# Low parts of every fourth weight chunk by an adding transfer, and a 128-row low part of the rotary key

## The chip, the cores and the metric

The kernel runs on one core of a Trainium2 chip. The metric is the device time of one execution in microseconds (us). A core has a matmul engine (TensorE, PE in the rows; its weight loads are PEld), VectorE (DVE), ScalarE (ACT), GpSimd (POOL) and SyncE (SP, which here only issues loads); 16 DMA engines move data between HBM and the on-chip memory SBUF. Matmuls write to PSUM, from where VectorE or ScalarE take the result.

## The reference

A two-layer encoder trunk on 256 tokens of width 2048, all in float32. Cut to what matters:

```python
for l in range(DEPTH):                                   # DEPTH = 2
    proj = rms_norm(x, attn_norm[l]) @ w_in[l]           # 2048 x 4928
    aq, ak, av, bq, bk, bv, cq, ckv, ckr = split(proj)
    ya = dense_block_attention(rope(aq), rope(ak), av)   # 6 heads, 2 key heads
    yb = dilated_mixture(rope(bq), rope(bk), bv)         # 4 heads, 3 patterns
    q  = rms_norm(cq) @ w_uq[l]                          # 6 heads, 128 + 64 rotary columns
    kv = rms_norm(ckv) @ w_ukv[l]                        # 6 heads, 128 key + 128 value columns
    k  = concatenate([k_nope, broadcast(apply_rope(ckr))])   # one rotary key of 64 for all heads
    yc = dense_block_attention(q, k, cv)                 # scores over 192 columns
    x  = x + concatenate([norm(ya), norm(yb), norm(yc)]) @ w_out[l]
    x  = x + conv_ffn(rms_norm(x), w_up[l], ..., w_down[l])  # 2048 -> 2 x 5632 -> 2048
return rms_norm(x, final_norm)
```

## The kernel before

**Two parts for each operand.** TensorE multiplies in float32r, which keeps fewer bits than float32. So each operand is held as a high part (the value rounded to float32r) and a low part (value minus high part), and a product is made of three: high x high, high x low, low x high. Activations live in `pg` tiles (high and low side by side), weights in `wh` and `wl`.

**Weight chunks.** All weights of both layers are streamed through the core once, in 802 chunks of at most 128 x 1024 numbers (512 KB; most of w_out's and a third of w_down's are 384 KB), in the order of PLAN: w_in (78 chunks a layer), w_ukv, w_uq (11), w_out (40), w_up and w_down (176 and 96, interleaved in four groups). For each chunk there are three steps: `emit_dma` issues the load into a landing tile `wland` on SyncE's queue, `emit_high` casts it to `wh` on ScalarE, `emit_low` subtracts `wh` from `wland` into `wl` on VectorE. Buffers rotate: 5 of wland (LAND), 4 of wh (SPLIT + 1), 3 of wl (SPLIT). Each engine works its queue in order.

**Who is ahead of whom.** `use()` is called when TensorE's code comes to a chunk u. It first calls `prefetch`, which writes out the cast of chunk u+3, the low part of chunk u+2 and the load of the chunk five behind the low parts. The cast of u+3 writes the wh buffer of chunk u−1, and the low part of u+2 the wl buffer of u−1, so both wait for TensorE to be done with that; the load waits for the low part that frees its landing tile.

**How chunks are used.** `rows` (w_in, values, rotary queries): weights are the moving operand, two k-blocks of 512 columns a chunk; the second matmul of a chunk already reads wl. `cols` (w_out, w_down, the 128-wide heads): weights are stationary; for each half of the chunk first all matmuls with wh, then those with wl. `up` (w_up): eight matmuls with wh, then eight with wl. Results go to one of two `mm` accumulators in PSUM.

**The order of the rest.** Everything else (norms, rotary embedding, heads, convolution) is written as generators that `pump` advances between the matmuls of a chunk, when the planner's clock (class Clock, a model of each engine's time) says that what they need is done. `urgent` ones come first, attention heads (`bg`) after them.

**Group C's scores.** `ckr_gen` makes the rotary key: its transposed 64 rows stand twice in the 128 rows of `krh` (high part), while `krl` (low part) has 64 rows. The rotary query tile `qr` has its high part in rows 0 to 63 and its low part in rows 64 to 127. One matmul with krh gives high x high plus low x high; a second one, with the first 64 rows of qr and krl, gives high x low. With the three products of the 128 other columns, that is five matmuls of 256 columns for each head and each block of 128 queries.

**Lines.** All compute instructions are recorded through one helper and carry line 164 (L164); loads carry L270. `rstd` puts a power of −0.5 on GpSimd (tiles `small`), which has little else to do.

Of the kernel before, what the change touches and what calls it, by code (L numbers as in the profile page):

```python
# [14 lines left out]
F32 = mybir.dt.float32  # L15
F32R = mybir.dt.float32r
BF16 = mybir.dt.bfloat16
AF = mybir.ActivationFunctionType
ALU = mybir.AluOpType
AX = mybir.AxisListType  # L20

P = 128
D = 2048
S = 256
# [8 lines left out]
ROPE_C = 64  # L33
# [9 lines left out]
CHUNK = 1024  # L43
# [15 lines left out]
def plan():  # L59
# [3 lines left out]
    def cols(mat, ks, c0, w):  # L63
        for run in k_runs(ks, w):
            out.append((mat, run, c0, w))
# [53 lines left out]
class Clock:  # L119
# [9 lines left out]
    def run(self, engine, cost, outs, ins):  # L129
        start = max([self.at[engine]] + [self.written.get(i, 0.0) for i in ins])  # L130
        end = self.at[engine] = start + cost
        for o in outs:
            self.written[o] = end + self.HOP
        for x in outs + ins:
            self.last[x] = max(self.last.get(x, 0.0), end + self.HOP)
        self.step = max(self.step, end + self.HOP)
# [84 lines left out]
class Kern:  # L221
# [51 lines left out]
        c.written.setdefault(dst.name, c.at["dma"] + 2000.0)  # L273


    LAND, SPLIT = 5, 3

    def emit_dma(self):
        i = self.n_dma
# [11 lines left out]
    def emit_high(self):  # L291
        i = self.n_high
        _, _, nk, w = self.chunks[i]
        sz = nk * w
        h = self.t("wh", [P, CHUNK], self.SPLIT + 1, F32R)
        if i > self.SPLIT:
            self.clock.at["act"] = max(self.clock.at["act"], self.ends[i - self.SPLIT - 1])
        self.ac.copy(h[:, :sz], self.land[i][:, :sz])
        self.high[i] = h
        self.n_high += 1  # L300

    def emit_low(self):
        i = self.n_low
        _, _, nk, w = self.chunks[i]
        sz = nk * w
        lo = self.t("wl", [P, CHUNK], self.SPLIT, F32R)
        h = self.high.pop(i)
        if i >= self.SPLIT:
            self.clock.at["dve"] = max(self.clock.at["dve"], self.ends[i - self.SPLIT])
        self.ve.tensor_tensor(lo[:, :sz], self.land.pop(i)[:, :sz], h[:, :sz].bitcast(F32), ALU.subtract)  # L310
        v = lambda x: x[:, :sz].rearrange("p (k n) -> p k n", k=nk)
        self.parts[i] = (v(h), v(lo))
        self.n_low += 1
# [393 lines left out]
    def attention(self, layer, act, norm):  # L707
# [9 lines left out]
        def uses(n, *tiles):  # L717
            for t in tiles:
                used[id(t)] = [t, n]

        def used_once(*tiles):
            for t in tiles:
                used[id(t)][1] -= 1
                if used[id(t)][1] == 0:
                    self.pg.put(t)
# [9 lines left out]
        qn, qr, kn, vC = {}, {}, {}, {}  # L735
# [26 lines left out]
        def ckr_gen(pm1):  # L762
            while "ckv" not in state:
                yield
            t = state["ckv"]
            self.evac(pm1, t[:, :, 256:], rs[0], 256)
            k = self.t("ckr", [P, NB, 1, ROPE_C], 1)
            self.evac(pm1, k[:, :, 0], rs[0], ROPE_C, 256)
            self.mm.put(pm1)
            yield  # L770
            ss = self.small(2)
            yield from self.sumsq(t, ss)
            tmp, z = yield from self.rope(k, self.c3("cosC"), self.c3("sinC"), 32, True)
            yield
            r = self.rstd(ss, 512, 2)
            yield
            self.scale(t, r)
            yield
            g = vec("c_kv_norm", 4)
            yield from self.transposed(lambda j, b: t[:, b, j * P:(j + 1) * P], 0, ckvT,  # L780
                                       [g[:, j:j + 1] for j in range(4)])
            self.tm.put(t)
            pt = yield from self.take(self.at)
            for b in range(NB):
                self.te.transpose(pt[:, 0, b * P:(b + 1) * P], z[:, b, 0].rearrange("p s d -> p (s d)"), self.ident)
            self.scr.put(tmp)
            yield
            h, lo = self.kr
            self.ac.copy(h, pt[:, 0])
            self.ve.tensor_tensor(lo, pt[:ROPE_C, 0], h[:ROPE_C].bitcast(F32), ALU.subtract)  # L790
            self.at.put(pt)
            kr.append(self.kr)

# [43 lines left out]
        def c_heads():  # L837
            for i in range(3):
                while not (i in qn and i in qr and i in kn and i in vC and kr):
                    yield  # L840
                mine = (*qn[i], qr[i], *kn[i], *vC[i])
                uses(2, *mine)
                (qh, ql), (kh, kl), (rh, rl) = qn[i], kn[i], kr[0]
                for j in range(2):
                    h = 2 * i + j
                    parts = [(x[:, j], y[:, j]) for x, y in ((qh, kh), (qh, kl), (ql, kh))]
                    parts += [(qr[i][:, j], rh), (qr[i][:ROPE_C, j], rl)]
                    self.bg.append(self.head(parts, (HD + ROPE_C) ** -0.5, vC, (i, j), outs["C"], 10 + h,
                                             lambda mine=mine: used_once(*mine)))

# [112 lines left out]
        product(act, K16, 512, lambda pm: a_gen(True, pm))  # L963
        product(act, K16, 256, ckv_gen)
        product(act, K16, 320, ckr_gen)
        product(act, K16, 512, cq_gen, True)
        for hs in ((0, 1), (2,)):
            product(ckvT, K4, 256 * len(hs), lambda pm, hs=hs: vC_gen(hs, pm))
        for i in range(3):
            pm = self.take_mm()  # L970
            self.cols(pm, ckvT, K4, i == 2)
            self.urgent.append(nope_gen(kn, i, pm))
        product(cqT, K4, 384, qr_gen)
        self.urgent.append(c_heads())
        for i in range(3):
            pm = self.take_mm()
# [143 lines left out]
    def run(self):  # L1120
        nc, a = self.nc, self.a
        cp = self.cp
        self.x = [cp.tile([P, 2, S], F32, name=f"x{m}") for m in range(KD // 2)]
        self.cst = cp.tile([P, NCST], F32, name="cst")
        self.vecs = cp.tile([P, DEPTH * NVEC], F32, name="vecs")
        self.mask = cp.tile([P, NB, 512], BF16, name="mask")
        self.load(nc.scalar, self.vecs[:, :64], a["vecs"][:, :64])
        while self.n_dma < self.LAND:
            self.emit_dma()
        self.ident = self.cst[:, CST["ident"]:CST["ident"] + P]  # L1130
        self.ones = self.cst[:, CST["ones"]:CST["ones"] + P]
        self.half = self.cst[:, CST["half"]:CST["half"] + 16]
        self.kr = cp.tile([P, S], F32R, name="krh"), cp.tile([ROPE_C, S], F32R, name="krl")
        self.hs = Fixed(cp.tile([P, 2, S + 2], F32, name=f"hs{i}") for i in range(2))
        for h in self.hs.tiles:
            nc.gpsimd.memset(h[:, :, 0:1], 0.0)
            nc.gpsimd.memset(h[:, :, S + 1:S + 2], 0.0)

        act, norm = {}, self.new_norm()
        first = norm  # L1140
        g0 = VEC["attn_norm"]

        def each(step):
            for m in range(KD // 2):
                yield from step(m)

        self.urgent.append(each(lambda m: self.x_parts(m, act, self.vecs[:, g0:g0 + 16])))
        self.urgent.append(each(lambda m: self.add_squares(first, self.x[m])))
        def tables():
            while self.n_dma < len(self.x) + 1:  # L1150
                yield
            self.load(nc.sync, self.cst, a["cst"])
            self.load(nc.sync, self.vecs[:, 64:], a["vecs"][:, 64:])
            self.load(nc.sync, self.mask, a["mask"].rearrange("p (b k) -> p b k", b=NB))
            self.rope_gains(0)

        self.urgent.append(tables())
        for layer in range(DEPTH):
            if layer:
                self.rope_gains(layer)  # L1160
            self.urgent.append(self.rstd_rows(norm))
            fact, fnorm = self.attention(layer, act, norm)
            act, norm = self.ffn(layer, fact, fnorm, layer == DEPTH - 1)
        self.urgent.append(self.rstd_all(norm, False))
        self.drain(lambda: not self.urgent and not self.bg)
        r = norm.all[0].unsqueeze(1).to_broadcast([P, 2, S])
        for m, x in enumerate(self.x):
            self.ve.tensor_tensor(x, x, r, ALU.mult)
            nc.sync.dma_start(a["out"][m].rearrange("p (j s) -> p j s", j=2), x)
# [94 lines left out]
```

## Time and profile before

| | |
|---|---|
| median of 3 runs | 2286.99 us (2286.73 to 2287.81) |
| profiled execution | 2286.59 us, of which the span from first to last instruction is 2284.8 |
| TensorE busy | 2263.7 us, 99% |
| VectorE busy | 1644.1 us, 72% |
| ScalarE busy | 1217.7 us, 53% |
| GpSimd busy | 32.9 us, 1% |
| loads | 408 MB, 52.4% of the 16 DMA engines' span |

Busy times are sums over the span. Ends of matmuls are modelled and successive matmuls overlap, so the pace of TensorE is read from the starts of its instructions, and what holds it from the waits. A row of the timeline merges equal instructions that follow each other: its first two numbers are the start of the first and the time to the end of the last, xN their count, and in brackets the engine's idle time before it and what ended that.

### The profile page before, as it was taken

To read this page: it belongs to the slowest core of one execution; us is meant where nothing else is said; L and a number is where in the kernel's file an instruction comes from. 1 tells how busy PE (TensorE), PEld (TensorE's weight loads), DVE (VectorE), ACT (ScalarE), POOL (GpSimd) and SP (SyncE) were. 2 spreads that over 40 slices of the span, in tenths; PEclk is the share of its full clock that TensorE was granted. 3 is DMA by queue.
4 is the path that set the end of the run, shared out by engine and by line. 5 is a ranking of instruction groups with operands and counts; after the bars stand their busy time and mean duration, and the time that the engine had idled before them with its cause. 6 is when DMAs were issued, how large, how long until landed. Compare 5 with 4: busy or idle time off the path is not lost. (4 is left out here: it accounts for less than half of the span.)

```text
span 2284.8 us, 34786 instructions
## 1 busy us (share of the span) xinstructions
PE 2263.7 (99%) x13452; PEld 2009.3 (88%) x13452; DVE 1644.1 (72%) x2369; ACT 1217.7 (53%) x1778; POOL 32.9 (1%) x51
## 2 busy tenths in 40 slices
PE   8999999999999999999999999999999999999997
PEld 7889889888888888888988898898888888888897
DVE  6577778777766776776756877787777677667755
ACT  6456745555544554553545566555555455445543
POOL 1000000000000000000010000000000000000000
PEclk9999999999999999999999999999999999999999
DMA  7544435555555555555554444465555555555553
GB/s 275 183 147 149 161 116 189 193 185 191 186 180 198 187 186 190 191 181 186 191 188 173 157 148 140 136 198 185 188 190 184 185 194 191 181 194 191 182 186 121
DMA packets 119110, 410.15 MB, mean 180 GB/s; under 512 B 13344, under 2 KB 13856, under 8 KB 118944
## 3 DMA queue, kind: packets, MB, share of 16 engines
q1 hardware_dynamic: 118800, 407.90, 52.4%
q8 instruction: 105, 1.72, 0.3%
q14 instruction: 61, 0.50, 0.1%
q10 hardware_dynamic: 144, 0.03, 0.0%
HBM read 405.78 MB, written 2.10 MB: 179 GB/s over the span
## 5 line engine op out<-in xcount | busy, mean ns | idle before, releaser
L164 DVE TENSOR_TENSOR wl<-wland,wh 128x1024 fp32r<-128x1024 f32 (+2 forms) x802 | 943.6, 1177 | 497.3 <-PE mm L164 448.0
L164 PE MATMUL mm<-pg,wh 128*128 128x512 f32 (+1 forms) x5472 | 1274.1, 368 | 0.4 <-DVE pg L164 0.4
L164 ACT CAST wh<-wland 128x1024 fp32r<-128x1024 f32 (+2 forms) x802 | 810.7, 1011 | 761.3 <-PE mm L164 399.7
L164 PEld LDWEIGHTS mm<-pg,wh 128*128 128x128 f32 x5472 | 905.6, 190 | 120.0 <-PE mm L164 0.7
L164 PEld LDWEIGHTS mm<-pg,wl 128*128 128x128 f32 x4832 | 690.2, 190 | 60.3
L164 PE MATMUL mm<-pg,wl 128*128 128x256 f32 x4832 | 724.4, 282 | 0.0
L164 PE MATMUL mm<-wh,pg 128*128 128x512 f32 (+3 forms) x1504 | 435.9, 366 | 6.4 <-ACT pg L164 6.4
L164 PEld LDWEIGHTS mm<-wh,pg 128*128 128x128 f32 x1504 | 272.7, 189 | 46.6 <-ACT pg L164 6.4
L164 PE MATMUL mm<-wl,pg 128*128 128x512 f32 (+3 forms) x752 | 272.6, 362 | 0.3 <-DVE wl L164 0.2
L164 DVE SCALAR_TENSOR_TENSOR pp<-hs,vecs,pp 128x256 f32<-128x256 f32 x352 | 162.3, 482 | 6.3
L164 PEld LDWEIGHTS mm<-wl,pg 128*128 128x128 f32 x752 | 142.7, 190 | 19.8 <-DVE wl L164 1.2
L164 DVE TENSOR_TENSOR x<-x,mm 128x512 f32<-128x512 f32 x160 | 109.2, 683 | 6.9 <-PE mm L164 4.7
L164 ACT ACTIVATE pp<-hs,vecs 128x256 f32<-128x256 f32 x176 | 96.2, 594 | 15.5 <-DVE hs L164 15.5
L164 ACT CAST pg<-pp 128x256 fp32r<-128x256 f32 x88 | 35.8, 407 | 89.6 <-DVE pp L164 89.5
L164 ACT ACTIVATE pp<-pp 128x256 f32<-128x256 f32 x88 | 36.9, 419 | 86.7 <-DVE pp L164 86.7
L164 DVE TENSOR_TENSOR pg<-pp,pg 128x256 fp32r<-128x256 f32 x88 | 37.4, 425 | 38.7 <-ACT pg L164 38.7
L164 DVE TENSOR_TENSOR hs<-hs,rall 128x512 f32<-128x512 f32 x88 | 60.9, 692 | 3.1
L164 DVE TENSOR_TENSOR hs<-mm,hs 128x512 f32<-128x512 f32 x88 | 60.1, 683 | 0.0
L164 ACT COPY hs<-mm 128x512 f32<-128x512 f32 x88 | 51.1, 580 | 0.0
L164 PE MATMUL at<-pg,pg 128*128 128x256 f32 (+1 forms) x288 | 43.4, 294 | 0.0
L164 PEld LDWEIGHTS at<-pg,pg 128*128 128x128 f32 x288 | 38.3, 192 | 3.4 <-DVE pg L164 0.4
L164 POOL TENSOR_TENSOR small<-small,cst 128x2 f32<-128x2 f32 (+1 forms) x19 | 19.0, 1004 | 1480.4 <-DVE small L164 1480.4
(87 smaller groups left out, 790.8 us busy)
## 6 DMA issues: line engine op xcount, KB each, us to landing
wland<-in_w_up SPq DMA_DIRECT2D x352, 512.0 KB, 3.5
wland<-in_w_in SPq DMA_DIRECT2D x144, 512.0 KB, 3.5
wland<-in_w_down SPq DMA_DIRECT2D x128, 512.0 KB, 3.6
wland<-in_w_out SPq DMA_DIRECT2D x64, 384.0 KB, 3.0
wland<-in_w_down SPq DMA_DIRECT2D x64, 384.0 KB, 3.1
wland<-in_w_out SPq DMA_DIRECT2D x16, 512.0 KB, 3.5
wland<-in_w_ukv SPq DMA_DIRECT2D x12, 512.0 KB, 3.4
wland<-in_w_in SPq DMA_DIRECT2D x8, 480.0 KB, 3.2
```

The lines of the kernel that those rows point to most:

```text
L164: return f(*args, **kw)
```

## The change

Every fourth chunk from chunk 11 on (198 of the 802) gets its low part in another way. ScalarE, right after its cast, writes the landed weights with factor −1 into the wl tile, rounded to float32r, that is the negated high part. Then a transfer issued by GpSimd reads the same weights from HBM a second time and adds them onto the tile. VectorE has nothing to do for that chunk. There are now four wl buffers and four wland buffers (before: three and five). Besides, krl gets 128 rows, of which the lower 64 are set to zero once, and its matmuls use all 128 rows of qr.

```diff
-    LAND, SPLIT = 5, 3
+    LAND, SPLIT = 4, 3
+    BY_DMA = 4
...
         self.n_high += 1
+        if i >= 2 * self.BY_DMA and i % self.BY_DMA == self.BY_DMA - 1:
+            self.low_by_dma(i)
+
+    def low_by_dma(self, i):
+
+        while self.n_low < i:
+            self.emit_low()
+        mat, off, nk, w = self.chunks[i]
+        sz = nk * w
+        lo = self.t("wl", [P, CHUNK], self.SPLIT + 1, F32R)
+        h = self.high.pop(i)
+        self.ac.activation(lo[:, :sz], self.land.pop(i)[:, :sz], AF.Copy, scale=-1.0)
+        self.nc.gpsimd.dma_start(lo[:, :sz], self.a[mat][off:off + P * sz].rearrange("(p f) -> p f", p=P),
+                                 accum_op=ALU.add)
+        v = lambda x: x[:, :sz].rearrange("p (k n) -> p k n", k=nk)
+        self.parts[i] = (v(h), v(lo))
+        self.n_low += 1
...
-        lo = self.t("wl", [P, CHUNK], self.SPLIT, F32R)
+        lo = self.t("wl", [P, CHUNK], self.SPLIT + 1, F32R)
...
-            self.ve.tensor_tensor(lo, pt[:ROPE_C, 0], h[:ROPE_C].bitcast(F32), ALU.subtract)
+            self.ve.tensor_tensor(lo[:ROPE_C], pt[:ROPE_C, 0], h[:ROPE_C].bitcast(F32), ALU.subtract)
...
-                    parts += [(qr[i][:, j], rh), (qr[i][:ROPE_C, j], rl)]
+                    parts += [(qr[i][:, j], rh), (qr[i][:, j], rl)]
...
-        self.kr = cp.tile([P, S], F32R, name="krh"), cp.tile([ROPE_C, S], F32R, name="krl")
+        self.kr = cp.tile([P, S], F32R, name="krh"), cp.tile([P, S], F32R, name="krl")
+        nc.gpsimd.memset(self.kr[1][ROPE_C:].bitcast(F32), 0.0)
```

How the queues stand now, at two places. The first is ScalarE's queue late in w_up of layer 0 (about 992 to 1001 us of the profile), the casts of chunks 348 to 351 and what stands between; `hs`, `pp` and `pg` belong to the convolution. Before:

```order
L164 CAST wh_9686<-wland_9585 128x1024
L164 COPY hs_96<-mm_9580 128x2x256
L164 CAST wh_9711<-wland_9610 128x1024
L164 ACTIVATE pp_9721<-hs_96,vecs 128x256 x2
L164 ACTIVATE pp_9740<-pp_9721 128x256
L164 CAST wh_9742<-wland_9641 128x1024
L164 CAST pg_9757<-pp_9740 128x256
L164 CAST wh_9768<-wland_9667 128x1024
```

After:

```order
L164 CAST wh_9774<-wland_9693 128x1024
L164 COPY hs_94<-mm_9667 128x2x256
L164 CAST wh_9795<-wland_9724 128x1024
L164 ACTIVATE pp_9805<-hs_94,vecs 128x256 x2
L164 ACTIVATE pp_9824<-pp_9805 128x256
L164 CAST wh_9826<-wland_9753 128x1024
L164 CAST pg_9841<-pp_9824 128x256
L164 CAST wh_9852<-wland_9755 128x1024
L164 ACTIVATE wl_9856<-wland_9755 128x1024
L164 CAST wh_9880<-wland_9799 128x1024
```

The cast of chunk 351 (wh_9768 before, wh_9852 after) is now followed by an ACTIVATE from its landing tile into wl, ahead of the next cast; the rest has kept its order. VectorE's queue at the same place, the low parts of chunks 348 to 352 among the convolution's steps. Before:

```order
L164 TENSOR_TENSOR wl_9713<-wland_9585,wh_9686 128x1024
L164 SCALAR_TENSOR_TENSOR pp_9721<-hs_96,vecs,pp_9721 128x256 x4
L164 TENSOR_TENSOR wl_9744<-wland_9610,wh_9711 128x1024
L164 TENSOR_TENSOR pp_9740<-pp_9740,pp_9721 128x256
L164 TENSOR_TENSOR pg_9757<-pp_9740,pg_9757 128x256
L164 TENSOR_TENSOR wl_9770<-wland_9641,wh_9742 128x1024
L164 TENSOR_TENSOR wl_9793<-wland_9667,wh_9768 128x1024
L164 TENSOR_TENSOR hs_95<-mm_9685,hs_95 128x2x256
L164 TENSOR_TENSOR hs_95<-hs_95,rall_4353 128x2x256
L164 TENSOR_TENSOR wl_9818<-wland_9690,wh_9791 128x1024
```

After:

```order
L164 TENSOR_TENSOR wl_9797<-wland_9693,wh_9774 128x1024
L164 SCALAR_TENSOR_TENSOR pp_9805<-hs_94,vecs,pp_9805 128x256 x4
L164 TENSOR_TENSOR wl_9828<-wland_9724,wh_9795 128x1024
L164 TENSOR_TENSOR pp_9824<-pp_9824,pp_9805 128x256
L164 TENSOR_TENSOR pg_9841<-pp_9824,pg_9841 128x256
L164 TENSOR_TENSOR wl_9854<-wland_9753,wh_9826 128x1024
L164 TENSOR_TENSOR hs_93<-mm_9773,hs_93 128x2x256
L164 TENSOR_TENSOR hs_93<-hs_93,rall_4384 128x2x256
L164 TENSOR_TENSOR wl_9903<-wland_9799,wh_9880 128x1024
```

The subtraction of chunk 351 (the one that reads wland_9667 before) is gone, and the other four stand where they stood. The second place is GpSimd's queue in the first attention stage, late in w_in and at the start of w_ukv, which before held only the `small` operations of the norms (after):

```order
L314 DMA wl_1458<-in_w_in 128x1024
L164 TENSOR_TENSOR small_1523<-small_1521,cst 128x8
L164 TENSOR_TENSOR small_1536<-small_1534,cst 128x2
L314 DMA wl_1632<-in_w_in 128x1024
L314 DMA wl_1773<-in_w_in 128x1024
L314 DMA wl_1900<-in_w_in 128x1024
L164 TENSOR_TENSOR small_1960<-small_1958,cst 128x8
L314 DMA wl_2047<-in_w_in 128x960
L314 DMA wl_2233<-in_w_in 128x1024
L164 TENSOR_TENSOR small_2380<-small_2378,cst 128x2
L314 DMA wl_2389<-in_w_in 128x1024
L314 DMA wl_2514<-in_w_ukv 128x1024
```

Each `DMA wl` is an adding transfer, which waits for ScalarE's copy; the small operations of the norms now stand between them.

## Rows read from the trace of the kernel before

**Rows 1.** The page: engine, busy us (share of the span), instructions.

```profile
PE 2263.7 (99%) x13452; PEld 2009.3 (88%) x13452; DVE 1644.1 (72%) x2369; ACT 1217.7 (53%) x1778; POOL 32.9 (1%) x51
```

**Rows 2.** TensorE's waits: who waited for whom, us in total, times, longest.

```profile
PE mm L164 <- ACT pg L164: 6.4, 1, 6.4
...
PE mm L164 <- DVE wl L164: 0.2, 1, 0.2
```

**Rows 3.** Stretches: from:to, length, busy us by engine (instructions), PE clock, DMA share, GB/s.

```profile
0.00:57.00 57.00, 50.33 (x216) 40.87 (x217) 38.04 (x59) 35.69 (x51) 8.04 (x21) 1.00 0.79 275
...
1542.00:2000.00 458.00, 458.00 (x2624) 402.56 (x2623) 338.96 (x456) 242.98 (x334) 0.00 (x0) 1.00 0.54 187
...
2270.00:2285.00 15.00, 2.44 (x14) 1.86 (x12) 7.05 (x14) 1.54 (x3) 0.70 (x1) 0.63 0.38 140
```

**Rows 4.** Timeline of TensorE: nine 128-row matmuls; then group C's scores.

```profile
118.90 1.23 PE L164 MATMUL at<-pg,pg 128*128 128x256 f32 x9
...
286.33 0.38 PE L164 MATMUL at<-krl,pg 64*128 64x256 f32 x1
286.64 0.61 PE L164 MATMUL at<-pg,pg 128*128 128x256 f32 x3
287.09 0.28 PE L164 MATMUL at<-krh,pg 128*128 128x256 f32 x1
287.30 0.38 PE L164 MATMUL at<-krl,pg 64*128 64x256 f32 x1
```

**Rows 5.** Groups by shape: xcount, busy us, mean ns, idle before by releaser.

```profile
L164 DVE TENSOR_TENSOR wl<-wland,wh 128x1024 fp32r<-128x1024 f32 x658 | 804.8, 1223 | 403.3 <-PE mm L164 365.3 <-issue 15.3 <-ACT pp L164 10.8
...
L164 ACT CAST wh<-wland 128x1024 fp32r<-128x1024 f32 x658 | 689.4, 1048 | 604.3 <-PE mm L164 276.6 <-issue 253.4 <-DVE x L164 55.5
```

**Rows 6.** Timeline of w_up, layer 0: chunk 351's cast to its use.

```profile
1000.35 1.05 ACT L164 CAST wh<-wland 128x1024 fp32r<-128x1024 f32 x1
1000.86 2.00 PE L164 MATMUL mm<-pg,wh 128*128 128x512 f32 x8
...
1009.24 2.00 PE L164 MATMUL mm<-pg,wh 128*128 128x512 f32 x8
...
1011.08 1.11 PE L164 MATMUL mm<-pg,wl 128*128 128x256 f32 x8
```

**Rows 7.** Timeline of w_in, layer 0: a cast, and later first matmuls with wl.

```profile
121.57 0.39 PE L164 MATMUL mm<-wl,pg 128*128 128x512 f32 x1
...
121.59 1.06 ACT L164 CAST wh<-wland 128x1024 fp32r<-128x1024 f32 x1 [2.14 <-issue]
...
124.29 0.39 PE L164 MATMUL mm<-wl,pg 128*128 128x512 f32 x1
...
131.71 0.39 PE L164 MATMUL mm<-wl,pg 128*128 128x512 f32 x1
```

**Rows 8.** Timeline of w_down, layer 1: a cast, and its chunk's matmuls with wl.

```profile
2183.80 1.05 ACT L164 CAST wh<-wland 128x1024 fp32r<-128x1024 f32 x1 [1.39 <-PE mm L164]
...
2192.60 0.63 PE L164 MATMUL mm<-pg,wl 128*128 128x256 f32 x4
```

**Rows 9.** Timeline of w_out, layer 1: a cast, and its chunk's matmuls with wl.

```profile
1505.58 0.84 ACT L164 CAST wh<-wland 128x768 fp32r<-128x768 f32 x1 [1.32 <-PE mm L164]
...
1512.90 0.52 PE L164 MATMUL mm<-pg,wl 128*128 128x256 f32 x3
```

**Rows 10.** The page: DMA queue (packets, MB, share); loads (count, KB, us to landing).

```profile
q1 hardware_dynamic: 118800, 407.90, 52.4%
...
wland<-in_w_up SPq DMA_DIRECT2D x352, 512.0 KB, 3.5
...
wland<-in_w_out SPq DMA_DIRECT2D x64, 384.0 KB, 3.0
```

**Rows 11.** Groups by shape: GpSimd's power of the norms.

```profile
L164 POOL TENSOR_TENSOR small<-small,cst 128x2 f32<-128x2 f32 x15 | 11.0, 730 | 1133.8 <-DVE small L164 1133.8
```

## The prediction

> **What bounds the kernel now.** I read the page's busy shares first: TensorE is busy 2263.7 of 2284.8 us, VectorE 72%, ScalarE 53% [rows 1]. A busy share alone says little, so the next view is the waits of TensorE, by whom it waited for. There the engine that the change relieves hardly appears: TensorE waited for a low part from VectorE once, 0.2 us [rows 2]. The table of stretches says where its 21.1 idle us lie: 6.7 in the first 57 us (the first weights and x arriving) and 12.6 in the last 15 (the final norm) [rows 3], which leaves about 2 us for everything between. Granted clock is 1.00 there. So the kernel runs at the pace at which matmuls start one after another, and only two things can move it: a change in that pace, or a new wait that TensorE does not have now. The last view is thus the timeline of TensorE at the place that the second half of the diff touches.
>
> **Padding the rotary low part: a change of pace, −9.1 us.** A score block of group C is five matmuls of 256 columns: three of 128 rows, one with krh (128 rows), one with krl (64 rows). Nine 128-row matmuls of 256 columns in a row take 1.23 us, the last of them 0.28 from start to end, so they start every (1.23 − 0.28) / 8 = 0.119 us [rows 4]. Around krl they do not: krh starts at 287.09, krl at 287.30 (0.21 later), and after the krl of 286.33 the next one starts at 286.64 (0.31 later). From krl to krl five matmuls take 287.30 − 286.33 = 0.97 us where five at 0.119 would take 0.59. The price of the 64-row operand is 0.38 us a block, and there are 2 blocks x 6 heads x 2 layers = 24. All of it lies on TensorE, which waits for nothing there, so padding to 128 rows gives 24 x 0.38 = 9.1 us. The padding adds one memset on GpSimd at the start, before TensorE has its first operand (6.4 us into the span), and no matmul: nothing to pay. If the slow start had another cause than the row count, the gain would be 0.
>
> **VectorE's share: 198 low parts go, worth nothing by themselves.** Chunks 11, 15, ... 799 are 198. A subtraction costs 1.22 us at full size [rows 5], so VectorE loses some 240 us of work. TensorE waited for such a result 0.2 us, so I count 0; at most the 2 us between the ends are to be had. ScalarE gains 198 negated copies. That operation is not in the trace; the nearest row is the cast of the same tile to the same type, 1.05 us [rows 5]: 208 us more, 62% of the span. Behind each copy on ScalarE's queue stand the next casts and evacuations; TensorE waited 6.4 us for ScalarE once, at the start [rows 2], and two PSUM accumulators cover a chunk's delay of 1.05 us, so 0 again.
>
> **The adding transfer: the step that decides.** Its result must land before the first matmul with that wl. The room comes from the timeline, stage by stage. The cast of chunk u+3 starts when chunk u−1's last high matmul is done, the negated copy follows it (1.05 us) and needs the wl buffer of chunk u−1, free by then; with 0.1 for the hand-over GpSimd can issue 1.15 us after the cast's end.
> - w_up: cast ends 1001.40, issue at about 1002.5; chunk u starts at 1000.86, u+3 at 1009.24, its low matmuls at 1011.08 [rows 6]. Room 8.5 us.
> - w_in: cast ends 122.65, issue 123.8; first low matmul of u at 121.57, one chunk is 124.29 − 121.57 = 2.72, so that of u+3 comes at 129.73 bare [rows 7]. Room 5.9; where attention work is put between, as here (the matmul comes at 131.71), 7.9.
> - w_down: cast ends 2184.85, issue 2186.0, first low matmul of u+3 at 2192.60 [rows 8]. Room 6.6.
> - w_out (384 KB chunks): cast ends 1506.42, the smaller copy 0.84, issue 1507.4, needed at 1512.90 [rows 9]. Room 5.5.
>
> What the transfer takes no row shows. Nearest are the plain loads of the same bytes: 3.5 us from issue to landing for 512 KB, 3.0 for 384 KB [rows 10]. The difference is 0.5 us per 128 KB, so 2.0 us of a full load is data and 1.5 is not. Adding has to read both the weights and the tile: estimate 1.5 + 2 x 2.0 = 5.5 us, and 1.5 + 2 x 1.5 = 4.5 for the small chunks. The lower bound is the plain load, 3.5. The upper: 1 us later start (GpSimd's small operations take 0.73 to issue and do [rows 11]) and one plain load ahead of it on the same 16 engines, 2.0: 8.5 us. I take 5.5, since bytes are what the rows scale with. It is under every room, by 0.4 in w_in and by 1.0 or more elsewhere: cost 0. The bounds stay for the range: at 3.5 still 0, at 8.5 see the rivals.
>
> The Trainium skill, "Collectives: The Full Stack", section "The bandwidth ceiling: the fold count and why AG ≠ RS ≠ AR", says that a transfer that adds runs at half rate because it reads two sources, not because of the addition; by that rule the estimate of 5.5 us stands as it is. The Trainium skill, "DMA: Bandwidth & Descriptors", section "Specifications", puts the first byte of a transfer issued by GpSimd at about 1 us against 0.6 for one from SyncE; by that the estimate would be 5.9 us, and the bare room of w_in would be used up to the last tenth. No row of before shows either.
>
> **What else moves.** Four landing buffers instead of five: a load is now issued four chunks before its cast, when the low part of chunk u+2 (or the negated copy) is done, about 1.2 us into chunk u, and its cast is due when chunk u+3 begins, three chunks or 8.4 us after u began [rows 6]: 7 us against 3.5. Loads busy the 16 DMA engines 52.4% of the span [rows 10]; 198 of 802 chunks read twice more add about 26 points, 78%, still under the whole. If that cover went, each late load would hold a cast and, three chunks on, TensorE. On GpSimd's queue the 15 small norm operations of 0.73 us [rows 11] can now stand behind a transfer that waits for ScalarE's copy, and VectorE's diag and the evacuations wait for them: up to 1 to 2 us each, covered by two accumulators of some 11 us each; the last norm comes after the last transfer. Sum: −9.1 + 0.
>
> **Rivals.**
> (A) Late transfers, slower than before. If landing takes longer than the room, TensorE stands still once in four chunks, and each stand adds fully, because the next cast hangs on TensorE. By stage there are 36 in w_in and 6 in w_ukv and w_uq (taken like w_in), 48 in w_down, 20 in w_out, 88 in w_up. At 7.0 us: 42 x 1.1 = 46 at the bare room, about half of it where attention work stretches the room; 48 x 0.4 = 19; w_out and w_up 0. So 42 to 65 us less 9.1: about 2330. At 8.5 us: 42 x 2.6 + 48 x 1.9 + about 20 x 1.2 = 224, at most 2502. The point from which the sign turns is about 6.3 us. For it: the loads in flight share the same engines, and a new issuer may start later. Against it: 5.5 by bytes, and half of the transfers are in w_up with 8.5 us.
> (B) Just late: 6.0 to 6.3 us, stands of 0.1 to 0.4 us on up to 42 chunks, 4 to 14 us, which eats the gain of the padding: about 2286.
> (C) The padding does nothing because the slow start has another cause, and the transfers fit: 2287. Against it: the 0.31 us stands right behind every 64-row matmul shown and behind no 128-row one.
>
> **How the numbers follow.** The profiled execution took 2286.59 (span 2284.8 and 1.8 around it); the median of the runs is 2286.99, 0.4 above. 2286.99 − 9.1 = 2277.9, predicted 2278. Chances: forecast 0.57; late transfers (A) 0.30; B 0.09; C 0.04. Within 0.2% is 2282.4 to 2291.6, about what a measurement of this kernel can tell from no change: faster 0.57, same 0.13, slower 0.30. Range: from 2274 (forecast plus the 2 us of idle time between, and some more from the blocks followed by 512-column matmuls) up into rival A to 2335, above which some 0.16 is left. The forecast's own range is 2274 to 2282.
>
> **What would show it.** Right: krl matmuls of 128 rows starting every 0.12 us; TensorE's waits without a row for wl; landing of the adding transfer 5 to 6 us; VectorE near 1405 us and ScalarE near 1425 busy. Wrong: a row "PE mm from DMA wl" or idle TensorE time before every fourth chunk (the transfer's landing then over 6), w_in first; or five-matmul blocks still at 0.97 us.

## Result: 5% slower, and the profile after

The changed kernel takes 2408.46 us (median of 3 runs, 2406.87 to 2416.61) against 2286.99 before: a ratio of 1.054 [1.0519, 1.0561]. The prediction was 2278, its range ended at 2335. The likeliest rival, late transfers, is what happened, and it cost more than the range allowed (the median of 7.8 us that the transfers took lies between the two cases that were priced, 7.0 and 8.5 us).

The page of the changed kernel, profiled at 2416.61 us with a span of 2414.8: busy us by engine, the two DMA queues that matter (packets, MB, share of 16 engines), and the issues (count, KB, median us to landing).

```profile
PE 2296.2 (95%) x13452; PEld 2014.0 (83%) x13452; DVE 1418.4 (59%) x2171; ACT 1408.3 (58%) x1976; POOL 207.4 (9%) x250
...
q1 hardware_dynamic: 118800, 407.90, 52.1%
q0 software_dynamic: 28512, 99.56, 23.3%
...
wland<-in_w_up SPq DMA_DIRECT2D x352, 512.0 KB, 4.6
...
wl<-in_w_up POOLq DMA_DIRECT2D x88, 512.0 KB, 8.1
...
wl<-in_w_in POOLq DMA_DIRECT2D x34, 512.0 KB, 8.0
wl<-in_w_down POOLq DMA_DIRECT2D x32, 512.0 KB, 7.3
```

Against [rows 1], VectorE lost 226 us of work, as meant, and ScalarE gained 191. TensorE is idle for 2414.8 − 2296.2 = 118.6 us where it was idle 21.1. The adding transfer takes 7.3 to 8.1 us in these rows, not 5.5, and the plain loads beside it went from 3.5 [rows 10] to 4.6. All 198 adding transfers together:

```profile
DMA to landing us min/median/max: 5.2/7.8/10.6
```

TensorE's waits say who ended the idle time (us in total, times, longest):

```profile
PE mm L164 <- DMA wl<-in_w_in: 37.5, 23, 4.4
PE mm L164 <- DMA wl<-in_w_down: 22.6, 25, 2.4
PE mm L164 <- DMA wl<-in_w_up: 18.2, 23, 1.9
PE mm L164 <- DMA wl<-in_w_out: 7.6, 9, 1.9
...
PE mm L164 <- DMA wl<-in_w_uq: 4.5, 2, 2.9
...
PE mm L164 <- DMA wl<-in_w_ukv: 1.5, 2, 1.0
```

Before had no row of this kind ([rows 2] has the only waits for wl there, on VectorE). They come to 91.9 us. Such a wait of TensorE between two matmuls is called a stand from here on. One of them, in w_in, from the timeline of the changed kernel (TensorE, ScalarE and GpSimd; the rows between are left out):

```profile
103.53 1.05 ACT L164 CAST wh<-wland 128x1024 fp32r<-128x1024 f32 x1 [3.60 <-PE mm L164]
...
104.49 1.05 ACT L164 ACTIVATE wl<-wland 128x1024 fp32r<-128x1024 f32 x1
...
105.83 0.86 POOL L314 DMA_DIRECT2D wl<-in_w_in  x1 [12.85 <-ACT wl L164]
...
111.22 0.61 PE L164 MATMUL mm<-wh,pg 128*128 128x512 f32 x2
...
114.02 0.80 PE L164 MATMUL mm<-wl,pg 128*128 128x512 f32 x1 [2.19 <-DMA wl<-in_w_in]
...
115.47 0.63 PE L164 MATMUL mm<-wl,pg 128*128 128x512 f32 x1
...
117.71 0.40 PE L164 MATMUL mm<-wl,pg 128*128 128x512 f32 x1
...
118.41 1.05 ACT L164 CAST wh<-wland 128x1024 fp32r<-128x1024 f32 x1 [5.72 <-PE mm L164]
```

Read it from the top. The cast ends at 104.58, the negated copy at 105.54, and GpSimd begins to issue at 105.83, 1.25 after the cast's end (1.15 was assumed). TensorE wanted the result 2.19 us before it got it, at 111.83. So the room (the time from the issue to the first matmul that needs the result) was 111.83 − 105.83 = 6.0 us, the bare 5.9 of the prediction; what didn't fit is the transfer, 8.2 us. The price doesn't end there. After the stand the matmuls of 512 columns take 0.63 to 0.80 us instead of 0.40, until 117.5. The next cast comes after 5.72 idle us of ScalarE. The same stretches as a table of the changed kernel (length, busy us of PE, PEld, DVE, ACT and POOL with their instructions, PE clock, DMA share, GB/s):

```profile
114.00:117.40 3.40, 3.38 (x8) 2.70 (x9) 0.00 (x0) 0.00 (x0) 0.00 (x0) 0.51 0.65 228
117.40:120.80 3.40, 3.40 (x16) 2.77 (x16) 0.00 (x0) 2.39 (x3) 0.09 (x1) 1.00 0.01 4
...
1542.00:2000.00 458.00, 447.53 (x2637) 392.52 (x2636) 288.20 (x428) 279.54 (x386) 38.60 (x43) 1.00 0.81 224
```

The granted clock was 0.51 for the 3.4 us behind the stand, which is the lower of the two levels (1.2 of 2.4 GHz): 8 matmuls instead of 16. In all, the trace after shows nine such drops inside the work, each behind a stand of 1.8 to 4.4 us, eight of them 3.4 us long and one 6.8; the trace before shows none there. Most stands, some of 2.0 to 2.4 us among them, had no drop behind them. The third row is the stretch of [rows 3] in which TensorE had no idle time at all (the changed kernel is some 95 us behind by then, so part of the work in it is another): now it is idle 10.5 of 458 us there, with the DMA engines at 81% instead of 54%.

### The profile page after: what moved, and what is told of

Same layout as the page of the kernel before. It is cut to its first block, busy times and chain, and to the rows that moved or that the text cites. A ratio compares the mean times of both kernels' runs of the same rounds, so it can differ in the third digit from the quotient of the medians.

```text
span 2414.8 us, 34922 instructions
## 1 busy us (share of the span) xinstructions
PE 2296.2 (95%) x13452; PEld 2014.0 (83%) x13452; DVE 1418.4 (59%) x2171; ACT 1408.3 (58%) x1976; POOL 207.4 (9%) x250
## 3 DMA queue, kind: packets, MB, share of 16 engines
q0 software_dynamic: 28512, 99.56, 23.3%
## 5 line engine op out<-in xcount | busy, mean ns | idle before, releaser
L164 DVE TENSOR_TENSOR wl<-wland,wh 128x1024 fp32r<-128x1024 f32 (+2 forms) x604 | 707.6, 1173 | 270.8 <-ACT wh L164 268.4
L164 PE MATMUL mm<-pg,wl 128*128 128x256 f32 x4832 | 734.1, 284 | 53.5 <-DMA wl<-in_w_down 22.6
L164 PE MATMUL mm<-wh,pg 128*128 128x512 f32 (+3 forms) x1504 | 442.3, 370 | 6.5 <-ACT pg L164 6.5
L164 PE MATMUL mm<-wl,pg 128*128 128x512 f32 (+3 forms) x752 | 279.1, 371 | 39.4 <-DMA wl<-in_w_in 37.5
L164 ACT ACTIVATE wl<-wland 128x1024 fp32r<-128x1024 f32 (+1 forms) x198 | 202.1, 1021 | 17.6 <-PE mm L164 17.3
L314 POOL DMA_DIRECT2D wl<-in_w_up x88 | 76.1, 864 | 926.2 <-ACT wl L164 770.8
L314 POOL DMA_DIRECT2D wl<-in_w_down x48 | 41.4, 862 | 492.5 <-ACT wl L164 438.0
L314 POOL DMA_DIRECT2D wl<-in_w_in x36 | 31.5, 874 | 414.2 <-ACT wl L164 339.8
```

What stands on the lines that cost most here:

```text
L164: return f(*args, **kw)
L314: self.nc.gpsimd.dma_start(lo[:, :sz], self.a[mat][off:off + P * sz].rearrange("(p f) -> p f", p=P), accum_op=ALU.add)
```

## Experiments

Times of before were 2286.84 and 2286.74 us beside these runs. Each diff is against the changed kernel where nothing else is said.

### 1. The padding alone

Against the kernel before:

```diff
-                    parts += [(qr[i][:, j], rh), (qr[i][:ROPE_C, j], rl)]
+                    parts += [(qr[i][:, j], rh), (qr[i][:, j], rl)]
...
-        self.kr = cp.tile([P, S], F32R, name="krh"), cp.tile([ROPE_C, S], F32R, name="krl")
+        self.kr = cp.tile([P, S], F32R, name="krh"), cp.tile([P, S], F32R, name="krl")
+        nc.gpsimd.memset(self.kr[1][ROPE_C:].bitcast(F32), 0.0)
```

> The kernel before with the 128-row low part of the rotary key alone; no transfer, buffers as before. The theory of the 64-row price: 24 blocks x 0.38 us = 9.1 us less than 2287.0, so 2277.9, and the five matmuls of a block in 0.59 us instead of 0.97. If the slow start around these matmuls has another cause: 2287.0.

Measured: 2279.73 us (2278.79 to 2279.94), 0.9967 [0.9955, 0.998]. The page and the timeline of TensorE in this kernel:

```profile
PE 2254.2 (99%) x13452; PEld 2006.2 (88%) x13452; DVE 1644.1 (72%) x2369; ACT 1217.5 (53%) x1778; POOL 32.1 (1%) x52
```

```profile
286.47 0.29 PE L164 MATMUL at<-krh,pg 128*128 128x256 f32 x1
286.59 0.28 PE L164 MATMUL at<-krl,pg 128*128 128x256 f32 x1
286.71 0.52 PE L164 MATMUL at<-pg,pg 128*128 128x256 f32 x3
287.07 0.29 PE L164 MATMUL at<-krh,pg 128*128 128x256 f32 x1
287.19 0.28 PE L164 MATMUL at<-krl,pg 128*128 128x256 f32 x1
```

From krl to krl now takes 287.19 − 286.59 = 0.60 us where [rows 4] had 0.97, and TensorE is busy 9.5 us less (2263.7 to 2254.2; 9.1 was the sum). The time fell by 7.1: TensorE's idle time rose from 21.1 to 23.5 us. The pace came as worked out; 2.4 us of it went into idle time elsewhere.

### 2. Everything but the transfer

```diff
-        self.nc.gpsimd.dma_start(lo[:, :sz], self.a[mat][off:off + P * sz].rearrange("(p f) -> p f", p=P),
-                                 accum_op=ALU.add)
```

> The changed kernel without the adding transfer itself: ScalarE's negated copy, the buffers (four landing tiles, four wl) and the padding stay; the weights are not added, so the low parts of 198 chunks are wrong. Theory A (the loss of 121 us is TensorE waiting for transfers that land after 7.8 us): all of it goes, 2278. Theory B (one landing tile fewer and 198 copies on ScalarE hold the casts): it stays well above, 2300 or more. Theory C (a second reading of the weights crowds the plain loads) expects 2278 here too.

Measured: 2285.42 us (2285.10 to 2287.24), 0.9994 [0.9985, 1.0003]. Its waits of TensorE:

```profile
PE mm L164 <- DVE pg L164: 5.1, 3, 2.5
PE at L164 <- DVE pg L164: 3.3, 4, 1.5
```

Padding alone has 0.3 and 2.6 us in these two rows. So 123 of the 129 us between padding alone and the changed kernel come with the transfer. The rest, 5.7 us, was counted as zero, in the prediction and in theory A here: these two rows grew by 5.5 us together, TensorE's waits for activations (`pg`) that come through VectorE and now stand behind the copies in ScalarE's queue. Experiment 6 takes the copies out.

### 3. The same transfers, which nobody reads

The copy and the adding transfer go into a tile of their own; VectorE makes all low parts as before, into three `wl` tiles.

```diff
-        lo = self.t("wl", [P, CHUNK], self.SPLIT + 1, F32R)
-        h = self.high.pop(i)
-        self.ac.activation(lo[:, :sz], self.land.pop(i)[:, :sz], AF.Copy, scale=-1.0)
+        lo = self.t("spare", [P, CHUNK], 1, F32R)
+        self.ac.activation(lo[:, :sz], self.land[i][:, :sz], AF.Copy, scale=-1.0)
...
-        v = lambda x: x[:, :sz].rearrange("p (k n) -> p k n", k=nk)
-        self.parts[i] = (v(h), v(lo))
-        self.n_low += 1
```

> The changed kernel in which the copy and the adding transfer go to a tile that nobody reads, and VectorE makes all 802 low parts as in the kernel before (three wl, four landing tiles; padding kept). The traffic of the change is all there, its wait is not. Theory A: 2278 to 2282, TensorE without waits for DMA. Theory C (crowding of the plain loads, 3.5 to 4.6 us each): casts wait for wland and most of the 121 us stays, 2380 or more. Theory B: 2300 or more.

Measured: 2293.86 us (2290.07 to 2296.03), 1.0029 [1.0019, 1.0038]. Its queue and issues:

```profile
q0 software_dynamic: 28512, 99.56, 26.0%
...
wland<-in_w_up SPq DMA_DIRECT2D x352, 512.0 KB, 4.9
...
spare<-in_w_up POOLq DMA_DIRECT2D x88, 512.0 KB, 7.5
```

The same 99.56 MB more, and the plain loads as slow as in the changed kernel (4.9 against 4.6), cost 8.4 us over experiment 2, where theory A had almost nothing (2278 to 2282). The other 115 of 123 us appear only when a matmul has to wait for the landing. So the crowding of the plain loads isn't the loss. That the plain loads make the landing longer is not excluded by this; the part on the prediction comes back to it.

### 4. A copy instead of an addition

The transfer overwrites the tile instead of adding to it (one read instead of two, all else alike).

```diff
-        self.nc.gpsimd.dma_start(lo[:, :sz], self.a[mat][off:off + P * sz].rearrange("(p f) -> p f", p=P),
-                                 accum_op=ALU.add)
+        self.nc.gpsimd.dma_start(lo[:, :sz], self.a[mat][off:off + P * sz].rearrange("(p f) -> p f", p=P))
```

> The changed kernel with the 198 transfers copying instead of adding (same issuer, tile, bytes and waits; wl then holds the whole weights, so the products with it are wrong). Tells how much of the 7.8 us is the second read. By the packets of the changed kernel: 2.8 us until the first packet, 4.7 us of packets, 0.4 after the last. Theory A1 (the start is what I had missed; a copy takes half of the packet time): landing about 2.8 + 2.4 + 0.4 = 5.6 us, TensorE waits under 10 us, 2278 to 2290. Theory A2 (adding itself is slow): landing near the plain loads' 4.6 us, 2278. If landing stays at 7 us or more, it is the issuer or the crowd: 2380 or more.

Measured: 2306.92 us (2305.87 to 2310.57), 1.009 [1.0076, 1.0104]. The page of this kernel, and then its instructions on `wl` (ns min/median/max, first and last start):

```profile
q0 software_dynamic: 28512, 99.56, 12.4%
...
wl<-in_w_up POOLq DMA_DIRECT2D x88, 512.0 KB, 5.6
...
wl<-in_w_in POOLq DMA_DIRECT2D x34, 512.0 KB, 5.3
```

```profile
L314 POOL DMA_DIRECT2D wl<-in_w_up x88: 527/527/572, 407.4 to 2148.8; - x88
...
DMA to landing us min/median/max: 3.7/5.5/7.7
```

A copy lands in 5.5 us, the very number that the prediction had for the addition, and then TensorE's waits for it are 7.3 (w_in), 2.4 (w_out) and 1.6 us (w_down). Adding makes the landing 2.3 us longer, and that is 101.5 us of time. The 2306.92 us lie above the 2278 to 2290 of theory A1, by the 8.4 us of traffic and 11.3 us of waits that it had not counted in full. Where the longer landing lies was read from the packets in the two traces (means of the 198): the first packet starts 3.0 instead of 2.6 us after the issue began, of which GpSimd's issue takes 0.86 instead of 0.53 us; from the first packet to the end of the last it takes 4.4 instead of 2.6 us (4.7 was the figure in the expectation); 0.4 pass from there to the landing in both.

### 5. The same transfers, issued one chunk earlier

The negated copy is made from the landed weights one chunk ahead, into two tiles of its own (`wa`). As room for them, `wl` keeps three buffers and `pg` has 37 tiles instead of 39.

```diff
+    def emit_neg(self, i):
...
+        lo = self.t("wa", [P, CHUNK], 2, F32R)
+        self.ac.activation(lo[:, :sz], self.land[i][:, :sz], AF.Copy, scale=-1.0)
...
+        self.neg[i] = lo
...
+        if i in self.neg:
+            self.land.pop(i)
+            self.parts[i] = (v(h), v(self.neg.pop(i)))
+            self.n_low += 1
+            return
...
+        i = u + 4
+        if 8 <= i < n and i % self.BY_DMA == self.BY_DMA - 1:
+            self.emit_neg(i)
```

> The changed kernel with the same 198 copies and adding transfers, but each issued one chunk earlier (for chunk u+4 at the start of u) into two tiles of their own, so that the copy does not wait for TensorE; the other low parts have three wl tiles, and two pg tiles are given up for the room. Theory A (landing of 7.8 us against the room): the room grows by a chunk, 2.8 us, to 8.7 in w_in, 9.4 in w_down, 8.3 in w_out and 11.3 in w_up, above the median landing everywhere; TensorE's waits for transfers fall from 92 to under 15 us and the time to that of the unread transfers, 2294, within 2285 to 2305. Theory C (the traffic itself): 2380 or more.

Measured: 2305.25 us (2299.75 to 2306.50), 1.0075 [1.0062, 1.0089]. Its issues, its waits of TensorE and those of ScalarE:

```profile
wland<-in_w_up SPq DMA_DIRECT2D x352, 512.0 KB, 5.1
...
wa<-in_w_up POOLq DMA_DIRECT2D x88, 512.0 KB, 7.9
```

```profile
PE mm L164 <- DMA wa<-in_w_in: 6.8, 5, 4.4
...
PE mm L164 <- DMA wa<-in_w_down: 2.6, 6, 1.2
...
PE mm L164 <- DMA wa<-in_w_uq: 1.1, 1, 1.1
```

```profile
ACT wh L164 <- DMA wland<-in_w_up: 23.4, 18, 3.1
...
ACT wa L164 <- DMA wland<-in_w_up: 16.3, 31, 2.7
```

The transfers are as many and nearly as slow (7.5 us in the median of all, against 7.8); their room grew by a chunk, some 2.8 us, beside which the 0.3 us are small, and 103 us are gone. This is the experiment that decides for landing against room. What is left above padding alone, 2305.25 − 2279.73 = 25.5 us, is about the sum of three prices already seen: 5.7 for the copies, 8.4 for the traffic, and 11.2 of waits for `wa` that are still there (rows of 0.4 and 0.3 us, for w_out and w_up, are left out above). ScalarE's new waits are for late plain loads, since they have one chunk less; they show no row on TensorE.

### 6 and 7. Two controls: the buffers, and 37 `pg` tiles

The first keeps the padding and the new buffer counts and leaves all low parts to VectorE; the second is padding alone with the `pg` tiles of experiment 5.

```diff
-        if i >= 2 * self.BY_DMA and i % self.BY_DMA == self.BY_DMA - 1:
-            self.low_by_dma(i)
```

> The padding and the new buffers (four landing tiles, four wl) without copies and transfers: VectorE makes all low parts. Splits the 5.7 us by which the kernel without the transfers (2285.4) stood above the padding alone (2279.7). If the landing tile is what is missed: 2285. If the 198 copies on ScalarE's queue are (they stand ahead of evacuations of the attention stage): 2279 to 2280, or a little less, since VectorE's subtractions no longer wait for a wl tile.

> The padding alone with 37 pg tiles instead of 39: the control for the kernel with earlier transfers, which gives up two. If the activations never need all 39: 2279.7, as the padding alone. If they do, TensorE waits for a tile in the attention stage: 2285 or more, and that much of the earlier transfers' time is not theirs.

Measured: 2279.19 us (2278.94 to 2279.86), 0.9966 [0.9954, 0.9979], and 2279.21 (2278.70 to 2279.93), 0.9966 [0.9954, 0.9978]. Both are padding alone. Four landing buffers instead of five cost nothing, so the 5.7 us of experiment 2 come with the copies on ScalarE, and two `pg` tiles fewer cost nothing either.

### 8. Half as many transfers

```diff
-    BY_DMA = 4
+    BY_DMA = 8
...
-        if i >= 2 * self.BY_DMA and i % self.BY_DMA == self.BY_DMA - 1:
+        if i >= 8 and i % self.BY_DMA == self.BY_DMA - 1:
```

> The changed kernel with every eighth chunk (99 instead of 198) by the adding transfer. Theory A: each late transfer stops TensorE on its own, so half of the 123 us between the changed kernel and the one without the transfers, and half of the copies' cost: about 2344. If the landing is long because the transfers and loads crowd each other (DMA share 0.65 instead of 0.76), less than half: 2295 to 2325.

Measured: 2358.81 us (2353.15 to 2365.23), 1.0315 [1.0295, 1.0336]. Its waits of TensorE:

```profile
PE mm L164 <- DMA wl<-in_w_in: 18.9, 11, 2.3
PE mm L164 <- DMA wl<-in_w_down: 14.9, 12, 2.0
PE mm L164 <- DMA wl<-in_w_up: 10.2, 12, 1.8
PE mm L164 <- DMA wl<-in_w_out: 8.1, 6, 1.9
```

99 transfers cost 79 us over padding alone, 198 cost 129: more than half, and more than either theory had (2344, or 2295 to 2325). So the loss doesn't follow how full the DMA engines are over the span (their adding queue fell from 23.3% to 12.0%). Each transfer by itself is late. Taken one by one in the two traces, the same 99 chunks stand 47 us in the changed kernel and 57 here, and their transfers land 0.21 us later (7.92 against 7.71 in the mean). Of these 99 transfers 91 met two or more plain loads in flight here and 75 in the changed kernel, which goes with the later landing (next section).

## Why the prediction failed, point by point

**The step that failed: "I take 5.5, since bytes are what the rows scale with".** With it the plain load that is ahead of the transfer on the same DMA engines, 2.0 us in the prediction's own upper bound, was left out of the sum, and the step ended in "under every room" and "cost 0". The landing measured 7.8 us (median of all 198). The 5.5 us are right for a transfer that meets nothing: in the traces of the changed kernel and of experiments 3, 5 and 8, six adding transfers of 512 KB were issued with no plain load in flight (issued and not yet landed when GpSimd's issue ended), and they landed after 5.3 to 5.7 us. Only one of them is in the changed kernel. Its other 163 of full size met one to three loads (means in us, from the beginning of the issue):

| loads in flight | transfers | first packet | first packet to end of last | landing |
|---|---|---|---|---|
| 0 | 1 | 1.6 | 3.4 | 5.3 |
| 1 | 38 | 2.3 | 4.8 | 7.5 |
| 2 | 111 | 3.2 | 4.5 | 8.1 |
| 3 | 14 | 3.8 | 4.6 | 8.7 |

So both parts of the landing grow when loads are in flight. That the sum of 5.5 met the bare transfer so well has some luck in it: the part that isn't data was 1.9 us, not 1.5, and the data part of the six 3.4 to 3.8, not 4.0. The new issuer itself costs little: two copies by GpSimd with no load in flight (experiment 4) landed after 3.7 and 3.8 us, where twelve loads by SyncE without another one beside them, in the kernel before, took 3.4 in the median.

The change brings the load and the transfer together by itself. The negated copy frees the landing tile for which the next load waits, so one event releases both. This is SyncE's row in the waits after (us in total, times, longest), and the load beside the stand shown above (start of the first of four):

```profile
SPq L270 <- ACT wl L164: 260.7, 149, 7.7
...
105.56 8.74 SPq L270 DMA_DIRECT2D wland<-in_w_in  x4
```

The load is issued at 105.56, the transfer at 105.83, its first packet starts at 108.26. In 193 of the 198 cases a load was issued in the half microsecond ahead of the transfer; in experiments 3 and 5, where the copy doesn't free the tile, it was 37 and 44, and the median landing was 7.1 and 7.5 us. This is read from the traces. No run holds the load back and leaves the rest alone, so how much of the time it would give back is not shown. The upper bound, 8.5, had this load in it, and held for the median, not for the longest landing (10.6).

On the second read of an adding transfer, the rows show: 99.56 MB took 23.3% of 2414.8 us on the DMA engines with addition and 12.4% of 2304.1 us as a copy, per transfer 2.84 and 1.44 us, a factor of 1.97. The Trainium skill, "Collectives: The Full Stack", section "The bandwidth ceiling: the fold count and why AG ≠ RS ≠ AR", puts the adding step of a collective at half rate because of its two sources; these two rows agree on the factor, and do not show whether the second read or the addition makes it. From the first packet to the last the factor is smaller, 3.4 to 3.8 us against 2.2 with no load in flight. The Trainium skill, "DMA: Bandwidth & Descriptors", section "Specifications", has about 1 us to the first byte of a transfer from GpSimd; here it was 1.6 us from the start of the issue, 0.86 of them the issue itself, with no load in flight, and 3.0 us in the mean of all 198; the measurement decides.

**The rooms were right.** w_in's bare room was 5.9 us by [rows 7] and 6.0 in the stand shown. So rival A could be priced with the measured landings: w_in, w_ukv and w_uq 42 x (8.0 − 5.9) = 88 at the bare room, half of that with attention work between; w_down 32 x (7.3 − 6.6) = 22 for its full chunks; w_out 20 x (6.4 − 5.5) = 18. That is 84 to 128 us; the waits came to 91.9. They are spread otherwise: w_up, with 8.5 us of room and a median landing of 8.1, still stood 23 times and 18.2 us, since landings reach 10.6. A median under the room was no cover.

**What the rival left out.** TensorE's idle time rose by 95.1 us over padding alone (118.6 against 23.5), its busy time by 42.0 (2296.2 against 2254.2). Each matmul held against the mean of its form in padding alone, some 16 of the 42 lie in the nine drops of the clock, and some 22 in the first matmul behind a stand, 0.27 us each for the 81 that lie outside of the drops: with nothing ahead of it to overlap with, its time counts in full (0.28 us for 256 columns, where matmuls that follow each other start every 0.12 us). These two are about two fifths on top of the waits of 91.9 us, and "each stand adds fully" did not have them.

**VectorE's relief: 0, right.** 226 us less work on VectorE show up nowhere in experiment 2, which is 6 us slower than experiment 6. **ScalarE's copies: 0, wrong by 5.7 us.** "Two PSUM accumulators cover a chunk's delay" looked at the evacuations; the late ones, by the waits of experiment 2, were the activations that go on through VectorE into `pg`. **Landing buffers: 0, right** (experiment 6). **GpSimd's queue:** no TensorE wait of any size leads back to its small operations. **DMA share:** 26 points were estimated, 23.3 measured.

**The padding: right.** −9.1 us was the sum, −9.5 of TensorE's busy time and −7.1 to −7.6 of the total came. Rival C fell.

In sum, from 2286.8: padding −7.1, copies +5.7, traffic +8.4, late landings with what they trail +114.6, to 2408.5. The padding alone, 2279.2 to 2279.7 us, is the best version found and beats both kernels.

## What to carry to other kernels

A transfer time worked out from its bytes is the time of a transfer that meets nothing. Before it is held against a room of a few microseconds, ask what the same event releases: here the copy that allowed the transfer also freed the tile for the next load, and the two met on the same DMA engines. Where the sum has a bound with that load in it, a forecast that needs the shorter time should stand on the bound, or the operation be measured first. Compare the room with the longest landing, not the median, and price a stand of the bound engine at more than its length, as the first matmul behind it and the clock follow. And work taken from an engine that nobody waits for is worth nothing, while its replacement can still cost.

## What the runs showed of the hardware

- Transfers issued by GpSimd, most of 512 KB, beside loads that busy the DMA engines half of the time, landed after 5.5 us as a copy and 7.8 us with addition (medians of 198); the issue held GpSimd 0.53 and 0.86 us. With no load in flight a full one took 3.7 to 3.8 us as a copy (two cases) and 5.3 to 5.7 with addition (six), and in the changed kernel 7.5, 8.1 and 8.7 us with one, two and three loads in flight.
- A packet of 4 KB took 0.174 us as a copy, 0.328 with addition, and 0.159 in a plain load (medians).
- Matmuls with an operand of 64 rows among ones of 128 rows cost 0.37 us for each change there and back (0.97 against 0.60 us for five of them).
- Behind a stand of 2.19 us the granted clock was 0.51 for 3.4 us. The nine drops inside the changed kernel's work each followed a stand of 1.8 to 4.4 us; other stands of 2.0 to 2.4 us had none behind them.
